# Respacing the state-space slots, a gelu on VectorE, and a new order at both ends of a one-core layer kernel

## The chip, the cores and the metric

The kernel runs on one core of a Trainium2 chip. The metric is the device time of one execution in microseconds (us). TensorE multiplies matrices, VectorE and ScalarE work elementwise, GpSimd is a slower elementwise engine, and SyncE (SP) issues nearly all DMA transfers from one queue. Each engine takes its instructions in a fixed order and waits on semaphores for the others.

## What is computed

One layer of a streaming encoder on 1024 prompt rows, 16 meta rows and 32 sample rows, all of width 1024, in fp32. The parts that matter here, cut from the reference:

```
xn = rmsnorm(h, norm_mix);  z = xn @ w_in            # q, kv, rope key | u | gate a | gate b
y_ssm, hr, hi = s5_scan(u, h0_re, h0_im)             # 64 groups, complex diagonal state, y = Re(C h) + D u
s = gelu(y_ssm)
o_b = (s @ w_glu_v) * sigmoid(s @ w_glu_g)
merged = sigmoid(g_a) * o_a + sigmoid(g_b) * o_b     # o_a: latent attention
h = h + merged @ w_out
h = h + relu(rmsnorm(h) @ w_mlp_up)**2 @ w_mlp_down
```

## The kernel before

Activations lie as columns: a tile has 128 features on the partitions and 1056 or 1072 positions along the free axis. Every fp32 operand of a large product is split into a high and a low fp32r part (`split`, lines 183 and 186: ScalarE casts the high part, GpSimd or VectorE subtracts for the low part), and `lin_part` (L264) makes three products of each pair: high x high, high x low, low x high.

**Input stage.** The string `HEAD` writes the order of the first steps out by hand. `xN` loads row tile N, `lN` loads weight block N, `i` loads the identity, `g` spreads the norm's gain over the partitions, `n...` makes the norms of the tiles named, `mN` scales tile N, `tNq` transposes half q of tile N and splits it, `w` splits the next weight block, and `pCM` makes the products of column chunk C with weight block M.

**State-space stage.** The remaining weight blocks of `w_in` are units (`run_unit`); a unit has eight k steps of nine products. Eight blocks j of four group pairs pass through the steps `st0` to `st5` in slots, one unit to a slot:

- `st0`: loads of U, a table tb on GpSimd, and tables clm (`cl`) and wxt (`wx`) on VectorE (48 instructions)
- `st1`: eight transposes of wxt (L581), copies to W, sixteen small products (L592), a store of ext and eight loads of M
- `st2`: products of U and W (L617), then VectorE's scan, from A (L638) to hb (L650, L651)
- `st3`: products of M and U (L668) and of hb and clm (L673) into Y, stores, and a load back as yt
- `st4`, `st5`: gelu of yt, and its store

`START[j]` is the slot of `st0` of block j; the others follow 1, 2, 4, 5 and 6 slots later. Steps written as generators give way after every few instructions, and `lin_part` takes one piece of each before every k step of the unit. Tiles with few buffers tie the blocks together: two of clm, one each of wxt, W, tb and hb.

The text's order is not the order that runs. The tile framework orders each engine's instructions by a timeline of its own, with the text's order as priority, so an instruction that it takes for ready can move ahead of its slot.

**Last stage.** The down projection works on pairs n of 256 output columns (`pairs`). For each, seven products `prod(n, p)` go into the PSUM banks X (two buffers), Z and Y (one each), and `gather` adds a bank to `yacc` on VectorE (L1635). The last four pairs (28 to 31) are written out one pair later: `out_rows` transposes eight blocks into the bank Y (L1646), ScalarE copies them to `yo` (L1649), and SP stores them (L1650); `out_sample` does the same for the sample rows (L1661, L1663).

Of the kernel before, what the change touches and what calls it, by code (L numbers as in the profile page):

```python
# [10 lines left out]
F32 = mybir.dt.float32  # L11
# [3 lines left out]
AF = mybir.ActivationFunctionType  # L15
ALU = mybir.AluOpType
# [98 lines left out]
KENG = ['vpvpvpp', 'vvpppvv', 'vpvvvvv', 'vpppvpp']  # L115


HEAD = "g x0 x8 x1 i l0 x2 x3 l1 x4 x5 x6 x7 n081 m0 t00 m8 t01 t80 m1 t10 w t11 w p00 p01 n23 m2 t20 t21 m3 t30 t31 p10 p11 n4567 m4 t40 t41 m5 t50 t51 p20 p21 m6 t60 t61 m7 t70 t71 p30 p31"
CH0 = [(0, 268), (268, 268), (536, 268), (804, 268)]
START = [2 + int(2.6 * j) for j in range(8)]  # L120
G3 = [(0, 3), (3, 3), (6, 2)]
GQ = [(t0 * KQ, nt * KQ) for t0, nt in G3]
EPS = 1e-6
# [2 lines left out]
GELU_C = math.sqrt(2.0 / math.pi)  # L126
# [30 lines left out]
def tile_layer(ctx: ExitStack, tc: tile.TileContext, a: dict, o: list, dbg=None):  # L157
    nc = tc.nc
# [140 lines left out]
    with tc.tile_pool(reuse_waits="tile", name="s5", bufs=1) as sp, tc.tile_pool(reuse_waits="tile", name="sps", bufs=3, space=PSUM) as sps:  # L299
# [32 lines left out]
        X = {}  # L332
        spare = iter([("M", 2)] * 2 + [("U", 2)] * 2 + [("Y", 3)] * 3 + [("A", 1), ("Bt", 1)])

# [45 lines left out]

        for w in HEAD.split():
            op, i = w[0], [int(c) for c in w[1:]]
# [28 lines left out]
        with ExitStack() as _:  # L411
# [14 lines left out]
            V = nc.vector  # L426
# [262 lines left out]
            def st4(j):  # L689
                yt = hold[j]["yt"]  # L690
                w = sp.tile([128, NQT], F32, tag="Y", name="gw", bufs=3)
                nc.scalar.activation(w, yt, AF.Square)
                V.tensor_scalar(w, w, GELU_C * 0.044715, GELU_C, op0=ALU.mult, op1=ALU.add)
                nc.gpsimd.tensor_tensor(w, w, yt, ALU.mult)
                hold[j]["w"] = w

            def st5(j):
# [4 lines left out]
                put("y", j, yt)  # L702
                put("s", j, w)

            slot = 2
            while slot <= START[7] + 6:
                steps = []
                for j in range(8):
                    for f, d in ((st5, 6), (st4, 5), (st3, 4), (st2, 2), (st1, 1), (st0, 0)):
                        if slot == START[j] + d:  # L710
                            steps.append(f(j))

                steps = [s for s in steps if s is not None]
                if w_units:
                    run_unit(*w_units.pop(0), steps)
                for s in steps:
                    for _ in s:
                        pass
                slot += 1
# [675 lines left out]
    with tc.tile_pool(reuse_waits="tile", name="mg", bufs=1) as mg:  # L1395
# [23 lines left out]
        for m in range(8):  # L1419
# [19 lines left out]
            for c0, n, ps in lin2(wh, wl, lambda k, c0, n: mh_[:, k, c0:c0 + n], lambda k, c0, n: ml_[:, k, c0:c0 + n], 8):  # L1439
# [4 lines left out]
                                               op0=ALU.mult, op1=ALU.subtract)  # L1444
# [19 lines left out]
    for g in range(3):  # L1464
        pt = tpp.tile([128, 512], F32, tag="tp", name="tp")
        b = blk[4 * g:4 * g + 4]
        for c0, n in b:
            i = c0 // 128
            nc.tensor.matmul(pt[:, c0 - 512 * g:c0 - 512 * g + n], lhsT=y[:n, i:i + 1].to_broadcast([n, 128]),
                             rhs=ident[:n, :n], start=True, stop=True)  # L1470
        w = sum(n for _, n in b)
# [20 lines left out]
    mu = ctx.enter_context(tc.tile_pool(reuse_waits="tile", name="mu", bufs=1))  # L1492
    hid = {}
# [58 lines left out]
    def w_load(n):  # L1552
        if n < len(pairs):
            g, j = pairs[n]
            for e in range(2):
                c0 = 256 * j + 128 * e
                nc.sync.dma_start(raws[2 * (n % 2) + e][:, :512].rearrange("p (k m) -> p k m", k=4),
                                  wd[512 * order[g]:512 * order[g] + 512, c0:c0 + 128].rearrange("(k p) m -> p k m", p=128))
# [36 lines left out]
    yps = ctx.enter_context(tc.tile_pool(reuse_waits="tile", name="yps", bufs=1, space=PSUM))  # L1595
# [17 lines left out]
    def bank2(pool, tag):  # L1613
        return pool.tile([128, 2, 512], F32, tag=tag, name=tag)

    def prod(n, p, ps, first, halves=((0, 1),)):
        g, j = pairs[n]
        e, wb, i = OPS[p]
        (h_, l_), x = whl[2 * (n % 2) + e], place[(7 * g + i) % 12]
        for hs in halves:  # L1620
            for k in range(2):
                for q, (w, u) in enumerate(((h_, 0), (h_, 1), (l_, 0))):
                    for s in hs:
                        nc.tensor.matmul(ps[:, s, :HS], lhsT=w[:, 256 * wb + 128 * k:256 * wb + 128 * k + 128],  # L1624
                                         rhs=x[:, u, k, HS * s:HS * s + HS],
                                         start=(first and k == 0 and q == 0), stop=(k == 1 and q == 2), skip_group_check=True)
        if j == 3:
            blk_load(7 * g + i + 12)

    def gather(n, r, c, ps, hs=None):  # L1630
        y_ = yacc[2 * pairs[n][1] + r][:, HN * c:HN * c + HN].rearrange("p (s n) -> p s n", s=2)
        v = ps[:, :, :HS]
        if hs is not None:
            y_, v = y_[:, hs:hs + 1], v[:, hs:hs + 1]
        nc.vector.tensor_tensor(y_, v, y_, ALU.add)  # L1635
# [4 lines left out]
    spot = [0]  # L1640

    def out_rows(m, t0, nt, pool=yps, tag="Y"):
        pt = bank2(pool, tag).rearrange("p a (b c) -> p (a b) c", c=128)[:, :nt]
        yv = yacc[m].rearrange("p (t c) -> p t c", t=T)
        for t in range(nt):
            nc.tensor.transpose(pt[:, t], yv[:, t0 + t, 0:128], ident)  # L1646
        spot[0] ^= 1
        yo = mu.tile([128, 8, 128], F32, tag=f"hid{spot[0]}", name="yo")[:, :nt]
        nc.scalar.activation(yo, pt, AF.Copy)  # L1649
        nc.sync.dma_start(y_o[:, t0:t0 + nt, m * 128:(m + 1) * 128], yo)  # L1650

# [24 lines left out]
    for n in range(N):  # L1676
        last = n == N - 1
        later = w_sums(n + 1) if not last else None
        X = bank2(xps, "X")
        prod(n, 1, X, True)  # L1680
        gather(n, 0, 0, X)
        if not last:
            w_split(n + 1, 0)
            later()
        if is_out(n - 1):
            out_rows(2 * pairs[n - 1][1], 0, 8)
        Z = bank2(zps, "Z")
        prod(n, 5, Z, True)
        if n == 0:

            rest[0]()
            gather(n, 1, 1, Z)
            Y = bank2(yps, "Y")
            prod(n, 2, Y, True)
            rest[1]()
            gather(n, 0, 0, Y)
            w_split(n + 1, 1)
            w_load(n + 3)
            prod(n, 6, X, False)
            gather(n, 0, 1, X)  # L1700
            rest[2]()
            prod(n, 3, Z, False)
            gather(n, 0, 1, Z)
            rest[3]()
            prod(n, 7, X, False)
            gather(n, 1, 1, X)
            before = X
            fill(n)
            continue
        gather(n, 1, 1, Z)  # L1710
        prod(n - 1, 4, before, False)
        gather(n - 1, 1, 0, before)
        if not last:
            w_split(n + 1, 1)
            w_load(n + 3)
        prod(n, 6, X, False)
        gather(n, 0, 1, X)
        if is_out(n - 1):
            out_rows(2 * pairs[n - 1][1] + 1, 0, 8)
        prod(n, 3, Z, False)  # L1720
        gather(n, 0, 1, Z)
        if is_out(n - 1):
            out_sample(n - 1)
        Y = bank2(yps, "Y")
        prod(n, 2, Y, True)
        gather(n, 0, 0, Y)
        prod(n, 7, X, False)
        gather(n, 1, 1, X)
        before = X
        if n < 3:  # L1730
            fill(n)
# [38 lines left out]
```

## Time and profile before

| | |
|---|---|
| median of 3 runs | 2052.73 us (2048.5 to 2053.4) |
| profiled execution | 2051.96 us, its span 2050.1 us |
| TensorE busy | 1992.4 us |
| VectorE, ScalarE, GpSimd busy | 1219.2, 765.8, 744.8 us |
| mean granted TensorE clock | 0.990 of full speed |

The span runs from the first to the last instruction of the profiled execution; the rest of its time lies around it. Busy time counts overlapping instructions of an engine once. The granted clock is the share of TensorE's full speed that the chip allowed.

### The profile page before, as it was taken

What the parts mean: (1) busy time and instruction counts of PE and PEld (TensorE: products, weight loads), DVE (VectorE), ACT (ScalarE), POOL (GpSimd) and SP (SyncE); (2) the same over time, 40 slices, a digit from 0 to 9 for tenths busy, and PEclk for the clock granted to TensorE, in tenths of its full rate; (3) what the DMA queues carried; (4) which work ended last, traced back from release to release, by engine and by line L of the source; (5) the groups of instructions that cost most, each with busy time, mean ns of one, the idle gap of its engine ahead of it and who ended that gap; (6) DMA issues with size and microseconds to landing.
All of it is one profiled execution on the core that took longest, in us unless ns stands there. A gap on an engine that the chain in (4) does not pass through costs nothing.

```text
span 2050.1 us, 35159 instructions
## 1 busy us (share of the span) xinstructions
PE 1992.4 (97%) x13328; PEld 1884.0 (92%) x13328; DVE 1219.2 (59%) x3092; ACT 765.8 (37%) x1691; POOL 744.8 (36%) x922
## 2 busy tenths in 40 slices
PE   7999999999999999999998999999999998999998
PEld 6988898899999888888887999999999998999997
DVE  5969776533756588988887444443444336444443
ACT  4213222223333467676765223333333332211112
POOL 0577676721222122121222001121221227767662
PEclk9999999999999999999999999999999999999999
DMA  5334444445343101110112634446555536765652
GB/s 146 115 110 126 126 132 131 122 128 184 120 150 118 55 12 27 18 28 17 24 20 87 196 102 126 132 153 225 200 207 224 196 141 236 293 241 195 250 197 85
DMA packets 269706, 276.62 MB, mean 135 GB/s; under 512 B 64602, under 2 KB 240433, under 8 KB 256994
## 3 DMA queue, kind: packets, MB, share of 16 engines
q1 hardware_dynamic: 269536, 274.38, 41.2%
q8 instruction: 105, 1.72, 0.3%
q14 instruction: 63, 0.52, 0.1%
q10 hardware_dynamic: 2, 0.00, 0.0%
HBM read 176.94 MB, written 97.39 MB: 134 GB/s over the span
## 4 chain that ended last, share of the span: by engine, by line
PE 82%; DVE 11%; DMA 3%; ACT 1%; POOL 1%; issue 1%; SPq 0%; ACTq 0%; DVEq 0%; POOLq 0%
PE acc L264 31%; PE pj L264 14%; PE X L1624 9%; PE Z L1624 4%; PE po L1279 3%; PE pj L1046 3%; PE pj L1111 3%; PE Y L1624 2%; PE pt L1254 1%; PE sp L673 1%; PE Sp L1197 1%; PE Sp L1189 1%; PE Sp L1190 1%; PE Sp L1192 1%; PE Sp L1191 1%
## 5 line engine op out<-in xcount | busy, mean ns | idle before, releaser
L186 POOL TENSOR_TENSOR wl<-raw,wh 128x1024 fp32r<-128x1024 f32 (+2 forms) x148 | 344.8, 2331 | 729.3 <-ACT wh L183 631.1
L183 ACT ACTIVATE wh<-raw 128x1024 fp32r<-128x1024 f32 (+2 forms) x166 | 169.1, 1019 | 696.9 <-PE acc L264 242.6
L264 PE MATMUL acc<-xh,wh 128*128 128x264 f32 (+6 forms) x736 | 189.3, 338 | 1.8 <-ACT xh L183 1.8
L264 PE MATMUL acc<-xh,wl 128*128 128x264 f32 (+4 forms) x736 | 181.5, 328 | 0.0
L264 PE MATMUL acc<-xl,wh 128*128 128x264 f32 (+5 forms) x736 | 181.5, 328 | 0.0
L1624 PE MATMUL X<-place,wh 128*128 128x264 f32 x1024 | 168.3, 287 | 2.1 <-ACT place L183 1.3
L1635 DVE TENSOR_TENSOR yacc<-X,yacc 128x528 f32<-128x528 f32 x129 | 90.4, 703 | 113.2 <-PE X L1624 113.0
L1624 PEld LDWEIGHTS X<-place,wh 128*128 128x128 f32 x1024 | 143.7, 191 | 2.7 <-ACT place L183 1.5
L264 PEld LDWEIGHTS acc<-xh,wh 128*128 128x128 f32 (+1 forms) x736 | 127.6, 191 | 14.3 <-issue 7.4
L264 PEld LDWEIGHTS acc<-xl,wh 128*128 128x128 f32 (+1 forms) x736 | 130.0, 190 | 2.1 <-issue 0.7
L264 PEld LDWEIGHTS acc<-xh,wl 128*128 128x128 f32 (+1 forms) x736 | 130.2, 191 | 1.9 <-issue 0.7
L1504 DVE SCALAR_TENSOR_TENSOR t<-acc,rstd 128x352 f32<-128x352 f32 x48 | 23.7, 522 | 150.5 <-PE acc L264 145.3
L1624 PE MATMUL X<-place,wl 128*128 128x264 f32 x512 | 104.7, 286 | 1.8 <-POOL wl L186 1.8
L264 PE MATMUL acc<-sh,wh 128*128 128x352 f32 x384 | 93.1, 325 | 0.6 <-ACT sh L749 0.6
L264 PE MATMUL acc<-sl,wh 128*128 128x352 f32 x384 | 93.6, 324 | 0.0
L264 PE MATMUL acc<-sh,wl 128*128 128x352 f32 x384 | 93.0, 324 | 0.0
L1624 PE MATMUL Z<-place,wh 128*128 128x264 f32 x512 | 84.5, 287 | 1.3 <-DVE yacc L1635 0.7
L1624 PEld LDWEIGHTS X<-place,wl 128*128 128x128 f32 x512 | 79.9, 190 | 2.0 <-POOL wl L186 2.0
L264 PE MATMUL pj<-ha,wh 128*128 128x352 f32 x360 | 79.1, 324 | 0.0
L264 PE MATMUL pj<-la,wh 128*128 128x352 f32 x360 | 78.7, 323 | 0.0
L264 PE MATMUL pj<-ha,wl 128*128 128x352 f32 x360 | 78.3, 323 | 0.0
L1279 PE MATMUL po<-ph,vt 128*128 128x256 f32 x320 | 74.3, 291 | 3.4 <-ACT ph L183 2.2
(483 smaller groups left out, 5294.4 us busy)
## 6 DMA issues: line engine op xcount, KB each, us to landing
bd<-place SPq DMA_DIRECT2D x49, 1056.0 KB
place<-bd SPq DMA_DIRECT2D x49, 1056.0 KB
raw<-in_w_mlp_up_dram SPq DMA_DIRECT2D x32, 512.0 KB
raw<-in_w_mlp_down_dram SPq DMA_DIRECT2D x64, 256.0 KB
raw<-in_w_in_dram SPq DMA_DIRECT2D x29, 512.0 KB
ud<-gst SPq DMA_DIRECT2D x8, 536.0 KB
U<-ud SPq DMA_DIRECT2D x64, 67.0 KB
yd<-Y SPq DMA_DIRECT2D x64, 66.0 KB
```

The source lines that it names most:

```text
L183: nc.scalar.activation(hi, src, AF.Copy)
L186: lo_eng.tensor_tensor(lo, src, hi.bitcast(F32), ALU.subtract)
L264: nc.tensor.matmul(pt[:M, :n], lhsT=w[:, k, :], rhs=x(k, c0, n), start=(k == 0 and p == 0), stop=(k == kt - 1 and p == 2),)
L673: nc.tensor.matmul(py[b][:, c], lhsT=cl[hs, q, pr, 1:9].rearrange("p a b -> p (a b)"), rhs=hb[hs, q, pr], start=False, stop=(q == 1),)
L1046: nc.tensor.matmul(ps[:R], lhsT=x[:, c, k0:k0 + R], rhs=w[:, c, :], start=(c == 0 and q == 0), stop=(c == 1 and q == 2))
L1111: nc.tensor.matmul(ps[:R, :384], lhsT=x[:, c, 128 * i:128 * i + R], rhs=w[:, c, :], start=(c == 0 and q == 0), stop=(c == 2 and q == 2))
L1189: nc.tensor.matmul(o_, lhsT=qh[:, h, 0, :R], rhs=kth[:, h, ks], start=True, stop=False)
L1190: nc.tensor.matmul(o_, lhsT=qh[:, h, 0, :R], rhs=ktl[:, h, ks], start=False, stop=False)
L1279: nc.tensor.matmul(po[:, :256], lhsT=w, rhs=x, start=st["first"], stop=(last and q == len(grp) - 1))
L1504: nc.vector.scalar_tensor_tensor(t, ps, 0.0, rstd[:, c], op0=ALU.max, op1=ALU.mult)
L1624: nc.tensor.matmul(ps[:, s, :HS], lhsT=w[:, 256 * wb + 128 * k:256 * wb + 128 * k + 128], rhs=x[:, u, k, HS * s:HS * s + HS], start=(first ...
L1635: nc.vector.tensor_tensor(y_, v, y_, ALU.add)
```

## The change

It does five things. `START` becomes 2, 5, 8, 10, 13, 15, 18, 20 (before: 2, 4, 7, 9, 12, 15, 17, 20). `st1` begins three k steps later in its slot when a step of an older block is in the same slot; in block 0, `st3` begins four k steps later and `st4` three. The inner gelu term is made by ScalarE (a square with a scale) and one VectorE instruction of two tensors, where it was a square, a VectorE instruction with two constants, and a GpSimd product. `HEAD` loads x2 ahead of weight block 0 and x4 ahead of block 1, and takes the second weight split behind the first products. In the last pair, product 2 goes ahead of product 6, and the row outputs rotate over three buffers instead of two.

```
-HEAD = "g x0 x8 x1 i l0 x2 x3 l1 x4 x5 x6 x7 n081 m0 t00 m8 t01 t80 m1 t10 w t11 w p00 p01 n23 ...
+HEAD = "g x0 x8 x1 i x2 l0 x3 x4 l1 x5 x6 x7 n081 m0 t00 t01 m8 m1 t80 t10 w t11 p00 w p01 n23 ...
...
-START = [2 + int(2.6 * j) for j in range(8)]
+START = [2, 5, 8, 10, 13, 15, 18, 20]
...
             def st4(j):
                 yt = hold[j]["yt"]
                 w = sp.tile([128, NQT], F32, tag="Y", name="gw", bufs=3)
-                nc.scalar.activation(w, yt, AF.Square)
-                V.tensor_scalar(w, w, GELU_C * 0.044715, GELU_C, op0=ALU.mult, op1=ALU.add)
-                nc.gpsimd.tensor_tensor(w, w, yt, ALU.mult)
+                nc.scalar.activation(w, yt, AF.Square, scale=math.sqrt(GELU_C * 0.044715))
+                V.scalar_tensor_tensor(w, w, GELU_C, yt, op0=ALU.add, op1=ALU.mult)
                 hold[j]["w"] = w
...
+            def late(n, f, j):
+                for _ in range(n):
+                    yield
+                yield from f(j) or ()
+
             slot = 2
             while slot <= START[7] + 6:
                 steps = []
                 for j in range(8):
                     for f, d in ((st5, 6), (st4, 5), (st3, 4), (st2, 2), (st1, 1), (st0, 0)):
                         if slot == START[j] + d:
-                            steps.append(f(j))
+
+                            n = 3 if f is st1 and steps else {st3: 4, st4: 3}.get(f, 0) if j == 0 else 0
+                            steps.append(late(n, f, j) if n else f(j))
...
-        spot[0] ^= 1
-        yo = mu.tile([128, 8, 128], F32, tag=f"hid{spot[0]}", name="yo")[:, :nt]
+        spot[0] = (spot[0] + 1) % 3
+        yo = mu.tile([128, 8, 128], F32, tag=("hid0", "hid1", "tA")[spot[0]], name="yo")[:, :nt]
...
         if not last:
             w_split(n + 1, 1)
             w_load(n + 3)
+        else:
+            Y = bank2(yps, "Y")
+            prod(n, 2, Y, True)
+            gather(n, 0, 0, Y)
         prod(n, 6, X, False)
         gather(n, 0, 1, X)
...
-        Y = bank2(yps, "Y")
-        prod(n, 2, Y, True)
-        gather(n, 0, 0, Y)
+        if not last:
+            Y = bank2(yps, "Y")
+            prod(n, 2, Y, True)
+            gather(n, 0, 0, Y)
         prod(n, 7, X, False)
         gather(n, 1, 1, X)
```

## Rows read from the trace of the kernel before

**Rows 1.** The page, part 1: busy us (share of the span) x instructions.

```profile
PE 1992.4 (97%) x13328; PEld 1884.0 (92%) x13328; DVE 1219.2 (59%) x3092; ACT 765.8 (37%) x1691; POOL 744.8 (36%) x922
```

**Rows 2.** Windows: stretch, length, busy us (instructions) by engine, granted clock, DMA share, GB/s.

```profile
0.00:25.00 25.00, 13.04 (x49) 9.30 (x50) 15.35 (x47) 16.84 (x29) 0.34 (x6) 1.00 1.01 263
131.95:137.00 5.05, 5.05 (x27) 4.33 (x27) 0.34 (x4) 0.52 (x3) 4.11 (x21) 0.53 0.31 78
250.00:258.00 8.00, 6.09 (x31) 5.58 (x29) 7.96 (x25) 1.86 (x5) 5.74 (x9) 0.79 0.33 135
381.00:389.00 8.00, 5.72 (x26) 5.35 (x25) 8.00 (x23) 3.24 (x6) 4.67 (x8) 0.81 0.16 66
400.00:500.00 100.00, 100.00 (x635) 94.45 (x634) 26.81 (x31) 28.18 (x57) 28.58 (x27) 1.00 0.44 136
```

**Rows 3.** TensorE's waits, whole span, last row 0 to 100: us, times, longest.

```profile
PE sp L581 <- DVE wxt L418: 5.4, 4, 2.3
PE sp L673 <- DVE hb L650: 4.2, 2, 4.0
...
PE sp L581 <- DVE wxt L418: 0.2, 1, 0.2
```

**Rows 4.** Timeline, block 0's scan and its reader: start, us, instruction [idle before].

```profile
117.56 1.29 DVE L638 TENSOR_TENSOR A<-xs,tb 128x1088 f32<-128x1088 f32 x1 [3.63 <-POOL tb L418]
...
131.95 0.81 PE L673 MATMUL sp<-hb,clm 64*128 64x132 f32 x4 [4.00 <-DVE hb L650]
```

**Rows 5.** Timeline of TensorE, slot of block 4's `st1` and block 3's `st3`.

```profile
252.20 0.33 PE L581 MATMUL sp<-ident,wxt 128*128 128x128 f32 x1 [1.91 <-DVE wxt L418]
...
257.46 0.72 PE L673 MATMUL sp<-hb,clm 64*128 64x132 f32 x8
```

**Rows 6.** Timeline of VectorE and GpSimd ahead of that.

```profile
241.84 2.84 DVE L693 TENSOR_SCALAR gw<-gw 128x1056 f32<-128x1056 f32 x1
...
245.80 2.48 DVE L416 TENSOR_TENSOR clt<-pw,bbar 128x128 f32<-128x128 f32 x1
...
255.75 0.16 DVE L651 TENSOR_TENSOR hb<-A,Bt 128x16 f32<-128x16 f32 x1
...
244.76 3.38 POOL L694 TENSOR_TENSOR gw<-gw,yt 128x1056 f32<-128x1056 f32 x1 [0.65 <-DVE gw L693]
```

**Rows 7.** Groups by form, VectorE, 60 to 420: busy us, mean ns, idle before.

```profile
L416 DVE TENSOR_TENSOR clt<-pw,bbar 128x128 f32<-128x128 f32 x32 | 17.2, 537 | 0.0
...
L700 DVE SCALAR_TENSOR_TENSOR gw<-gw,yt 128x1056 f32<-128x1056 f32 x6 | 7.4, 1240 | 0.0
```

**Rows 8.** Timeline of VectorE: first of block 5's 48 table instructions, and their successor.

```profile
266.49 0.62 DVE L418 TENSOR_TENSOR clm<-clt 128x144 f32<-128x144 f32 x2 [0.87 <-PE sp L673]
...
283.43 0.71 DVE L693 TENSOR_SCALAR gw<-gw 128x1056 f32<-128x1056 f32 x1
```

**Rows 9.** Timeline of ScalarE and VectorE in the input stage.

```profile
9.71 1.06 ACT L183 ACTIVATE wh<-raw 128x1024 fp32r<-128x1024 f32 x1 [0.68 <-DMA raw<-in_w_in_dram]
...
10.79 1.23 DVE L186 TENSOR_TENSOR wl<-raw,wh 128x1024 fp32r<-128x1024 f32 x1 [0.86 <-ACT wh L183]
...
12.78 1.28 DVE L363 SCALAR_TENSOR_TENSOR X<-X,r1y,gbc 128x1024 f32<-128x1024 f32 x1
```

**Rows 10.** The end: two copies of ScalarE's timeline, then the chain that ended last.

```profile
2032.72 1.03 ACT L1649 ACTIVATE yo<-Y 128x1024 f32<-128x1024 f32 x1 [8.22 <-PE Y L1646]
...
2040.92 1.02 ACT L1649 ACTIVATE yo<-Z 128x1024 f32<-128x1024 f32 x1 [4.64 <-PE Z L1646]
...
2037.23 1.73 PE Y L1624 x12
...
2039.75 1.11 PE Z L1646 x8
...
2042.60 3.88 DMA out_dram<-yo
2046.59 0.38 ACT yo L1649
```

More of the change, by code (lines that the diff above doesn't have):

```diff
@@ L115 @@
 KENG = ['vpvpvpp', 'vvpppvv', 'vpvvvvv', 'vpppvpp']
-HEAD = "g x0 x8 x1 i l0 x2 x3 l1 x4 x5 x6 x7 n081 m0 t00 m8 t01 t80 m1 t10 w t11 w p00 p01 n23 m2 t20 t21 m3 t30 t31 p10 p11 n4567 m4 t40 t41 m5 t50 t51 p20 p21 m6 t60 t61 m7 t70 t71 p30 p31"
+HEAD = "g x0 x8 x1 i x2 l0 x3 x4 l1 x5 x6 x7 n081 m0 t00 t01 m8 m1 t80 t10 w t11 p00 w p01 n23 m2 t20 t21 m3 t30 t31 p10 p11 n4567 m4 t40 t41 m5 t50 t51 p20 p21 m6 t60 t61 m7 t70 t71 p30 p31"
 CH0 = [(0, 268), (268, 268), (536, 268), (804, 268)]
-START = [2 + int(2.6 * j) for j in range(8)]
+START = [2, 5, 8, 10, 13, 15, 18, 20]
 G3 = [(0, 3), (3, 3), (6, 2)]
```

## The prediction

> **What bounds the kernel now.** The page comes first: TensorE is busy 97% of the span [rows 1]. Nothing in the change takes a product away, so it can win only what TensorE does not use: about 58 us of idle time in all, and the stretches in which its granted clock is low. The second view is the windows of the span [rows 2]. In a full stretch, 400 to 500 us, a product passes every 100 / 635 = 0.157 us at a granted clock of 1.00. In three stretches of the state-space stage the granted clock is under 1: 0.53 over 5.05 us, 0.79 over 8 and 0.81 over 8. That is the lower of two levels, 1.2 instead of 2.4 GHz, for part of each, and each stretch follows a TensorE wait. The third view says what those waits are [rows 3]: 5.4 us on wxt, VectorE's tables for the next block, before the transposes of `st1` (L581), and 4.2 us on hb, VectorE's scan result, before the output products of `st3` (L673). The reader is to see that a wait costs twice: once itself, and once in the slow clock after it. The price after it is 5.05 x 0.47 = 2.4, 8 x 0.21 = 1.7 and 8 x 0.19 = 1.5 us, 5.6 in all [rows 2].
>
> **Where the waits come from.** With `START` as it is, blocks 2, 4 and 7 come three slots after their predecessor, which itself came two after its own. In those places VectorE gets the predecessor's `st2` and the block's own `st0` in one stretch, and `st1` stands at the very head of the next slot. These are the three long wxt waits; a fourth, 0.2 us, belongs to block 0 and stays [rows 3]. The hb wait is nearly all block 0: VectorE starts its scan only when GpSimd's table is there, at 117.56, and TensorE stands 4.00 us until 131.95 [rows 4].
>
> **The new slots.** Only blocks 4 and 6 still come three slots after a pair that was two apart. Wherever an older block has a step in the slot, `st1` is put behind three k steps: 3 x 9 x 0.157 = 4.2 us at least [rows 2], more than any wxt wait (2.3 at most [rows 3]). In block 0 `st3` is put behind four k steps, 36 x 0.157 = 5.7 us; `st1` of block 1 moves from the slot before it into the same slot, which brings the slot's head forward by its eight transposes and sixteen small products: 8 x 0.33 = 2.6 us for the transposes by the longest row [rows 5], which overlap, so 2 us is my estimate for all. So hb is asked for some 3.7 us later against a wait of 4.00: gone within half a us. Removed: 5.4 + 4.2 - 0.2 = 9.4 of waits and 5.6 of slow clock, 15.0 us.
>
> **What is late next.** hb itself. In block 4's place the transposes got their tables at 252.20 after 1.91 us, and the old block's hb products followed at 257.46 [rows 5]; VectorE had written hb at about 255.9 [rows 6]. Without the wait and its slow clock TensorE would have come there 1.9 + 1.7 = 3.6 us sooner, at 253.9, 2 us before hb. Delaying `st1` alone would only hand the wait on. What may pull hb forward is the gelu edit. Its GpSimd product takes 3.38 us, and the VectorE instruction that starts inside it takes 2.48 [rows 6] where its kind has a mean of 0.54 [rows 7]: 1.9 us given back. VectorE pays 1.24 for the two-tensor form where the one-tensor form takes 0.71 undisturbed [rows 7, 8], so 0.5 more; it comes out 1.4 us ahead, hb at 254.5 against 253.9. The remaining wait is then 0.6 us in each of two places (blocks 4 and 6; the third place is gone). But the new form can be held up by GpSimd's weight splits as the old one was (2.84 in [rows 6]), and then it is 2 us with a slow clock of 1.6 behind it. Between 0.6 and 3.6 I take 1.5 each, 3 in all. State-space stage: 15.0 - 3 = 12 us gained; bounds 15 and 15.0 - 7.2 = 7.8.
>
> The row shows the one-tensor form at 0.71 and the two-tensor form at 1.24 us [rows 7, 8]. The Trainium skill ("VectorE: DVE Perf Modes", the perf-mode tier table) says that fp32 tensor-scalar work runs at twice the rate of any two-tensor operation; the trace agrees, 1.24 to 0.71. By that rule alone the gelu edit costs VectorE 8 x 0.53 = 4.2 us and gives nothing back, and hb comes later, not sooner: rival 1 below. The same skill ("SBUF — State Buffer", two separate sides) says that GpSimd and VectorE take turns at a shared port pair, a whole instruction at a time, which is what 2.48 beside 3.38 looks like; by that rule the edit pays.
>
> **Other moved steps.** What moves with `st0` of blocks 1, 2, 4 and 6 (eight loads of U each on SP, the tables on GpSimd) moves one slot, and is read two slots later. A later `st1` issues its store of ext and eight loads of M on SP's queue 4 us later; M is read three slots on, and a slot's 72 products alone take 11.3 us, so this is hidden. Its copies of W on ScalarE end some three k steps before the next slot reads them. `st4` of block 0 goes behind three k steps because yt now comes a little later; were it not, the weight casts behind it on ScalarE would wait. GpSimd loses eight products of 3.4 us, and the weight splits behind them come sooner; no TensorE wait in this stage names them, so I count nothing. The cover is the weight split one unit ahead; without it each would be a wait of up to 3.4 us.
>
> **Input stage.** Now ScalarE stands until 9.71 for the first weight block, and VectorE stands 0.86 us behind it and then makes that block's low part (1.23) in the middle of the norm that the first scaled rows need; those begin at 12.78 [rows 9]. The new order loads x2 before that block and x4 before the second, and splits the second block only behind the first products. If the split falls behind the norm, the first products come up to 0.86 + 1.23 = 2.1 us sooner; if the engines keep their order, all wait for a block that lands one load later, 512 KB at 263 GB/s, 2.0 us [rows 2]. VectorE has work without a pause after 12.78, so that only its idle 0.86 is likely to be won: I take 0.7.
>
> **The end.** The single "Y" bank passes from the rows of pair 30, copied from 2032.72 on, through their second half and the sample rows to the last pair's product 2, which starts only at 2037.23 [rows 10]. Every other product is done by then. Placed before the other two, it can start when that first copy ends, 2033.75: 3.5 us sooner. The next row transposes still queue behind it, and behind ScalarE's copies, so the copy that began at 2040.92 begins at about 2038.4: product and addition take 2039.75 - 2037.23 = 2.5 us and end at 2036.3, then come the other rows' transposes and copy, 1.0 each. Its store needs about 3.9 us [rows 10]; in the new rotation of three buffers the last copy waits for that store, the one before it for an older one. The copy that was at 2046.59 then starts at 2038.4 + 1.0 + 3.9 = 2043.3, 3.3 us sooner, and the last store goes with it. Bounds: 1 (the third buffer alone helps one copy) and 4.7 (the last copy too is free of its wait).
>
> **Sum.** 12 + 0.7 + 3.3 = 16.0 us. The profiled execution took 2051.96 (its span is 2050.1, 1.86 lie around it); the median of the runs shown is 2052.73, 0.8 above. 2051.96 - 16.0 = 2036.0. About 0.3%, 6.2 us, is what a measurement of this kernel can tell from no change.
>
> **Rivals.** (1) The waits only move: VectorE pays 0.5 us a block for the two-tensor form and gets nothing back, hb is late in the two places, something else in the third, each with its slow clock. Then block 0's 4.0 + 2.4 and the end's 3.3 remain: 2051.96 - 9.7 = 2042.3. For it speaks that hb stood 2 us behind wxt; against it the third pattern, which is gone. (2) The edits change little: the order in the trace is not that of the text alone (block 5's `st0` begins at 266.49 [rows 8], a slot and more ahead of its place), so new slots could give the old order. Then the end's 3.3 and small change remain: about 2048.5, within 0.3%. Against it: `st1` and `st3` stood exactly at their slots' heads. (3) Slower: block 1's tables. `st0` of block 1 now stands a slot behind `st2` of block 0. If VectorE takes them in that order it waits for GpSimd until 117.56, ends the scan at 131.95 [rows 4] and needs 17.0 us for the tables [rows 8], until 149; TensorE asks for them at about 129.5. A wait of 19.5 and 2 of slow clock make 2036 + 21.5 = 2057.5. It decides from a start of the tables later than 112.5, and makes the kernel slower once that start is some 14 us later still. Against it: VectorE has nothing else to do before 117.56, and wrote these tables ahead of their slot before.
>
> **How the numbers follow.** The forecast 0.64 (2030 to 2041), rival 1 0.15 (2040 to 2046), rival 2 0.12 (2046 to 2054), rival 3 0.09 (2054 to 2060). Faster 0.79, same 0.12, slower 0.09. The low end: 15 + 2.1 + 4.7 = 21.8 gained, 2030. The high end, 2047, takes in rival 1 and the top of the next and leaves out no more than 2 in 10.
>
> **What would show it.** Right: no wxt wait over 0.5 us behind block 0; no hb wait at block 0; a granted clock of 1.00 from 100 to 400 us; hb waits of 1 to 2 us at blocks 4 and 6 at most; product 2 of the last pair before the second row transposes; at most one long wait of ScalarE on a store at the end. Wrong: a new TensorE wait over 5 us at block 1 or 2, or the wxt waits at their old size.

## The result, and the profile after

The changed kernel takes 2036.78 us (median of 4 runs, 2033.65 to 2036.92) against 2053.05 for the kernel before on the same chip (4 runs, 2048.5 to 2053.4). The ratio is 0.9922 with a 95% interval of 0.9905 to 0.9939: faster, by 16.3 us or 0.8%. The forecast was 2036.0, with 2030 to 2047 as its range.

The page of the profiled execution (2036.92 us, span 2035.1, mean granted clock 0.996), its busy row, which answers to [rows 1]:

```profile
PE 1983.2 (97%) x13328; PEld 1878.1 (92%) x13328; DVE 1211.5 (60%) x3092; ACT 766.2 (38%) x1691; POOL 718.1 (35%) x914
```

TensorE makes as many products in 9.2 us less busy time: that is slow clock that is gone. GpSimd has eight instructions and 26.7 us less.

Three marks divide the span into parts that can be compared: the first transpose of ld (the end of the input stage), the first transpose of fin (the end of the state-space stage), and ScalarE's first copy of pair 30's rows. Before they stand at 52.10, 473.13 and 2032.72 us, after at 50.92, 458.81 and 2020.26. The parts, in us:

| | input stage | state-space stage | between | end |
|---|---|---|---|---|
| before | 52.10 | 421.03 | 1559.59 | 17.38 |
| after | 50.92 | 407.89 | 1561.45 | 14.84 |
| gained | 1.2 | 13.1 | -1.9 | 2.5 |

The windows view over the state-space stage of each kernel, before first (columns as in [rows 2]):

```profile
52.10:473.13 421.03, 411.30 (x2766) 379.42 (x2766) 283.05 (x699) 111.12 (x271) 264.92 (x465) 0.98 0.42 123
```

```profile
50.92:458.81 407.89, 404.85 (x2765) 376.37 (x2765) 276.40 (x699) 111.91 (x271) 238.19 (x457) 1.00 0.43 127
```

The length less TensorE's busy time is its idle time: 9.7 us before and 3.0 after. So the stage won 6.7 us of waits and 6.4 us of product time. The waits of TensorE after, from 50 to 475 us, against [rows 3]:

```profile
PE sp L673 <- DVE hb L650: 2.5, 1, 2.5
PE sp L581 <- DVE wxt L418: 0.5, 1, 0.5
```

One wait on hb is left, and it is not where the forecast put it. TensorE's timeline shows it at block 1, and the windows behind it show what it costs in clock:

```profile
173.28 0.72 PE L673 MATMUL sp<-hb,clm 64*128 64x132 f32 x8 [2.50 <-DVE hb L650]
```

```profile
173.28:179.00 5.72, 5.71 (x33) 5.12 (x34) 0.23 (x3) 0.00 (x0) 4.85 (x21) 0.70 0.15 64
179.00:184.00 5.00, 5.00 (x35) 4.50 (x35) 0.00 (x0) 1.17 (x3) 4.53 (x12) 1.00 0.43 116
```

5.72 x 0.30 = 1.7 us: part of that stretch went at 1.2 instead of 2.4 GHz. Everywhere else from 100 to 460 us the granted clock is 1.00, and at the places of blocks 4 and 6 TensorE waits for nothing.

### The profile page after: what moved, and what is told of

Read it like the earlier page. It is cut to its first block, busy times and chain, and to the rows that moved or that the text cites. A ratio compares the mean times of both kernels' runs of the same rounds, so it can differ in the third digit from the quotient of the medians.

```text
span 2035.1 us, 35117 instructions
## 1 busy us (share of the span) xinstructions
PE 1983.2 (97%) x13328; PEld 1878.1 (92%) x13328; DVE 1211.5 (60%) x3092; ACT 766.2 (38%) x1691; POOL 718.1 (35%) x914
## 4 chain that ended last, share of the span: by engine, by line
PE 88%; DVE 5%; DMA 3%; ACT 2%; POOL 1%; issue 1%; SPq 0%; ACTq 0%; DVEq 0%; POOLq 0%
PE acc L264 37%; PE pj L264 14%; PE X L1630 9%; PE Z L1630 4%; PE po L1285 3%; PE pj L1052 3%; PE pj L1117 3%; PE Y L1630 2%; PE pt L1260 1%; PE sp L673 1%; PE Sp L1203 1%; PE sp L617 1%; PE Sp L1195 1%; PE Sp L1196 1%; PE Sp L1198 1%; PE Sp L1197 1%
## 5 line engine op out<-in xcount | busy, mean ns | idle before, releaser
L1641 DVE TENSOR_TENSOR yacc<-X,yacc 128x528 f32<-128x528 f32 x129 | 90.4, 702 | 112.7 <-PE X L1630 112.5
```

## The experiments

The dispute is over which edit made the stage faster: the new slots with their delays, or the gelu edit, which the prediction used only to bring hb forward by 1.4 us. And for the gelu edit: is it the form of VectorE's instruction, or the GpSimd product that is gone? All runs are compared with the kernel before on the same chip. "Stage" is the state-space stage between the two marks; idle is its length less TensorE's busy time.

| kernel | time, us (runs) | stage | busy | idle | waits on wxt; hb |
|---|---|---|---|---|---|
| before | see above | 421.03 | 411.30 | 9.73 | 5.4; 4.2 |
| delays alone | 2049.07 (1) | 420.35 | 408.18 | 12.17 | 0.5; 5.0 |
| new slots and delays, old gelu | 2051.67 (10) | 416.65 | 407.44 | 9.21 | 0.5; 8.7 |
| gelu alone | 2042.06 (1) | 410.58 | 406.02 | 4.56 | 0.5; 4.0 |
| slots, delays and gelu | 2037.70 (4) | 407.80 | 404.73 | 3.07 | 0.5; 2.5 |
| new gelu and an idle GpSimd product | 2053.35 (10) | 417.21 | 407.02 | 10.19 | 6.0; 4.2 |
| old form, product on VectorE | 2044.92 (1) | 411.32 | 405.81 | 5.51 | 1.1; 4.4 |
| changed kernel | 2036.78 (4) | 407.89 | 404.85 | 3.04 | 0.5; 2.5 |
| changed kernel without delays | 2041.49 (1) | 411.61 | 405.33 | 6.28 | 0.5; 5.8 |
| changed kernel, `st3` of block 1 later | 2032.49 (5) | 403.36 | 402.83 | 0.53 | 0.5; 0 |

The times come from more than one chip, so that kernels are compared by their ratios to the kernel before and by the stage. A single time says little: in thirteen of the fourteen profiles (the last experiment says what is wrong with the other) the stretch "between", which no edit touches, takes from 1558.7 to 1564.3 us. The stage's length is steadier: the two kernels below that change only the last pair show 422.57 and 421.41 against 421.03.

**New slots and delays with the old gelu.** The new `START` and the delayed steps are in; gelu, load order and end are as before.

```
-START = [2 + int(2.6 * j) for j in range(8)]
+START = [2, 5, 8, 10, 13, 15, 18, 20]
...
+                            n = 3 if f is st1 and steps else {st3: 4, st4: 3}.get(f, 0) if j == 0 else 0
+                            steps.append(late(n, f, j) if n else f(j))
```

> The kernel before with the new slots and the delayed steps alone; the gelu keeps its GpSimd product, both ends stay old. If the gelu edit is what pulls hb forward (the prediction), hb is late without it: TensorE waits of 2 us or more on hb, each with its slow clock, at blocks 3 and 5 (read in the slots of blocks 4 and 6) and a longer one than 2.5 at block 1, so 2053 - 13 + 3 x 3 = about 2049. If the new slots alone do the work, the waits are those of the changed kernel, one of 2.5 us, and the time is 2053 - 13 = 2040.

2051.67 us, ratio 1.0001 (0.9989 to 1.0014): no change. TensorE's waits:

```profile
PE sp L673 <- DVE hb L650: 8.7, 3, 4.1
PE sp L581 <- DVE wxt L418: 0.5, 1, 0.5
```

The wxt waits are gone, and nearly the same time is now waited for hb, in three places: 4.12 us (block 1), 3.38 us (at 346.56) and 1.18 us (at 262.01), the last of them shorter than the 2 us that was expected. Without the gelu edit the slots only exchange one wait for the other. The profile's stage is 4.4 us shorter; the median of ten runs does not show it, and its interval of about 2.7 us either way has no room for it.

**The same with the new gelu.** Slots, delays and gelu; the ends are as before.

> The kernel before with the slots, the delayed steps and the gelu on VectorE; both ends stay old. By the changed kernel's trace the state-space stage gives 13 us: 2053 - 13 = 2040. If the input stage and the end carry more of the 16 us than the trace says (1.2 and 2.5), this stays above 2042.

2037.70 us, ratio 0.9937 (0.9922 to 0.9952). The stage, 407.80, and the waits, 2.5 on hb and 0.5 on wxt, are those of the changed kernel. So the stage's part of the change is these three edits, and the gelu edit decides what the other two are worth.

**The delays alone.** The old `START`, with the later `st1`, `st3` and `st4`.

> The kernel before with the delayed steps alone: old slots, old gelu. The prediction says that a later st1 only hands the wait on: no wxt wait over 0.5 us, block 0's hb wait gone, but hb waits of 1 to 2 us where wxt was late (blocks 1, 3 and 6), each with a slow clock; block 0's 6.4 us and little else are gained, about 2045. If the place of st1 was all, nothing takes the wxt waits' place: 2053 - 15 = 2038.

```profile
PE sp L673 <- DVE hb L650: 5.0, 4, 2.3
PE acc L264 <- ACT gst L309: 4.8, 1, 4.8
PE sp L617 <- DVE ext L599: 1.8, 1, 1.8
PE sp L581 <- DVE wxt L418: 0.5, 1, 0.5
```

The step "delaying `st1` alone would only hand the wait on" stands: wxt falls to 0.5, and hb in four places, ext and a bank that ScalarE had to empty take its place; 12.1 us in all, more than before. The stage is 0.7 us shorter. The wait of 4.8 us on that bank was in no expectation, and the one time is 4 us above the 2045 that was expected.

**Gelu alone.** Only the three lines of `st4`.

> The kernel before with the gelu on VectorE alone. If VectorE gets back more from GpSimd's missing product than the two-tensor form costs (1.9 against 0.5), the wxt waits of 1.0, 1.9 and 2.3 shrink by about 1.4 each and lose their slow clock, block 0's 4.0 stays: about 2053 - 4 - 3 = 2046. If VectorE only pays, the wxt waits grow by 0.5 each: 2054.

2042.06 us in one run, with 2050.24 for the kernel before (13 runs); the stage takes 410.58, 10.4 less than before. That is a larger gain than the 2046 that was expected. The waits:

```profile
PE sp L673 <- DVE hb L650: 4.0, 1, 4.0
PE sp L581 <- DVE wxt L418: 0.5, 1, 0.5
```

All three long wxt waits are gone, with the slots as they were; only block 0's wait on hb is left. This is the finding of the study: the edit that the forecast used as a helper does most of the work. VectorE's and GpSimd's timelines at block 4's place, the stretch of [rows 6], show how:

```profile
228.39 1.01 DVE L418 TENSOR_TENSOR clm<-clt 128x144 f32<-128x144 f32 x4 [15.76 <-PE sp L673]
...
238.22 1.23 DVE L693 SCALAR_TENSOR_TENSOR gw<-gw,yt 128x1056 f32<-128x1056 f32 x1
239.37 1.28 DVE L644 TENSOR_TENSOR_SCAN Gs<-L,A 128x544 f32<-128x544 f32 x1
240.57 2.42 DVE L416 TENSOR_TENSOR clt<-pw,bbar 128x128 f32<-128x128 f32 x1
...
246.56 0.28 DVE L418 TENSOR_TENSOR wxt<-clt 128x128 f32<-128x128 f32 x1
```

```profile
238.70 4.13 POOL L186 TENSOR_TENSOR wl<-raw,wh 128x1024 fp32r<-128x1024 f32 x1 [8.33 <-ACT wh L183]
```

From the first table instruction to the last of wxt VectorE needs 246.84 - 228.39 = 18.5 us. In the kernel before the same stretch runs from 230.78 to 252.14, 21.4. Of the 2.9 us, 1.6 are the gelu instruction itself (1.23 against 2.84 in [rows 6]) and 1.0 the first four table instructions (1.01 against 2.02 before). The instruction that the prediction counted on, the one of 2.48 us beside GpSimd's product [rows 6], is still held here, for 2.42: now by the weight split. At block 7's place it is not. VectorE's and GpSimd's rows there, the kernel before first, then gelu alone:

```profile
374.20 2.85 DVE L693 TENSOR_SCALAR gw<-gw 128x1056 f32<-128x1056 f32 x1
...
378.17 2.50 DVE L416 TENSOR_TENSOR clt<-pw,bbar 128x128 f32<-128x128 f32 x1
...
373.21 3.27 POOL L186 TENSOR_TENSOR wl<-raw,wh 128x1024 fp32r<-128x1024 f32 x1 [5.18 <-ACT wh L183]
...
377.12 3.39 POOL L694 TENSOR_TENSOR gw<-gw,yt 128x1056 f32<-128x1056 f32 x1 [0.65 <-DVE gw L693]
```

```profile
366.16 3.39 DVE L693 SCALAR_TENSOR_TENSOR gw<-gw,yt 128x1056 f32<-128x1056 f32 x1
...
370.67 0.26 DVE L416 TENSOR_TENSOR clt<-pw,bbar 128x128 f32<-128x128 f32 x1
...
365.11 3.32 POOL L186 TENSOR_TENSOR wl<-raw,wh 128x1024 fp32r<-128x1024 f32 x1 [5.11 <-ACT wh L183]
```

With gelu alone the gelu instruction stands beside the split, and the table instruction passes in 0.26 us. Block 2's place is like it (2.83 and 2.50 before, 3.39 and 0.26 with gelu alone). So in each of the three places two VectorE instructions were held before, one beside the weight split and one beside the product; without the product one is held, whichever the split meets. The two take 5.3 us together before and 3.65 after, at all three places: 1.7 us less, with the longer two-tensor form already paid. The whole stretches are 2.0, 2.9 and 2.8 us shorter at blocks 2, 4 and 7, where the wxt waits were 1.0, 1.9 and 2.3.

**The new gelu with an idle product.** GpSimd gets its work back, as two products of 480 columns each that nobody reads.

```
+                scr = sp.tile([128, 480], F32, name="scr", tag="scr")
+                for c in (0, 480):
+                    nc.gpsimd.tensor_tensor(scr, w[:, c:c + 480], yt[:, c:c + 480], ALU.mult)
```

> The kernel before with the gelu on VectorE, and GpSimd made to form two products of 480 columns (960 of the old 1056) from the same two tiles at the same place, into a tile that nobody reads. If GpSimd's product held VectorE up, VectorE gets its 2.2 us a block back no more, wxt comes late again (1 to 2 us in three places, each with a slow clock), and the time is 2042 + 8 = about 2050. If only the new form of VectorE's instruction counts, which is not held up behind a weight split (1.24 against 2.84), the wxt waits stay under 0.6 us and the time at 2042.

2053.35 us, ratio 1.0005 (0.9992 to 1.0018): by the time the whole gain is undone. The stage of the one profile, 417.21, is longer than with gelu alone by 6.6 us of the 10.4. TensorE's waits are those of before again:

```profile
PE sp L581 <- DVE wxt L418: 6.0, 4, 2.0
PE sp L673 <- DVE hb L650: 4.2, 2, 4.0
```

The same place in VectorE's and GpSimd's timelines:

```profile
241.13 3.39 DVE L693 SCALAR_TENSOR_TENSOR gw<-gw,yt 128x1056 f32<-128x1056 f32 x1
...
245.65 1.25 DVE L416 TENSOR_TENSOR clt<-pw,bbar 128x128 f32<-128x128 f32 x1
...
247.46 1.71 DVE L418 TENSOR_TENSOR wxt<-clt 128x128 f32<-128x128 f32 x3
```

```profile
240.42 2.99 POOL L186 TENSOR_TENSOR wl<-raw,wh 128x1024 fp32r<-128x1024 f32 x1 [5.46 <-ACT wh L183]
...
244.60 2.15 POOL L696 TENSOR_TENSOR scr<-gw,yt 128x480 f32<-128x480 f32 x1 [1.20 <-DVE gw L693]
```

Beside the two halves of the product, of 2.15 and 1.26 us, VectorE's table instructions stand again: 1.25 us where the same one passed in 0.26 at block 7 above, and 1.71 for the three that take 0.68 there.

The waits do not bring all of the slow clock back: over some 5 us behind the wxt waits at blocks 2, 4 and 7 (1.91, 1.84 and 2.04 us) the granted clock is 1.00, 0.67 and 1.00, where the kernel before has 1.00, 0.64 and 0.65. The windows behind block 7's wait, before first, then here:

```profile
384.58:389.00 4.42, 4.42 (x17) 4.42 (x18) 4.42 (x16) 0.60 (x1) 4.36 (x6) 0.65 0.29 119
```

```profile
383.04:388.00 4.96, 4.96 (x36) 4.44 (x38) 4.96 (x19) 0.60 (x1) 4.88 (x3) 1.00 0.27 109
```

So a wait does not always cost twice, and that is part of what this profile's stage keeps.

At block 4's place, in the rows above, the weight split began 0.71 us ahead of VectorE's gelu instruction, which then took 3.39 us; with gelu alone it began 0.48 us behind it, and it was the split that took longer, 4.13. The mean of the gelu instruction over its seven places is 2.17 us here, 1.86 with gelu alone and 1.55 in the changed kernel. The Trainium skill ("SBUF — State Buffer", two separate sides) says that of a VectorE instruction with two inputs in SBUF and a GpSimd one, the one that starts first has the shared port pair for its whole length and the other stands still; these two pairs of rows agree.

**The old form with the product on VectorE.** The one-tensor instruction stays, and VectorE makes the product that GpSimd made, so it bears one instruction more than before.

```
-                nc.gpsimd.tensor_tensor(w, w, yt, ALU.mult)
+                V.tensor_tensor(w, w, yt, ALU.mult)
```

> The kernel before with the old gelu's last product moved from GpSimd to VectorE: VectorE keeps the one-tensor instruction and gets a two-tensor one more, 1.24 us. If GpSimd's product was what held VectorE up (2.2 us), VectorE gains 1 us a block: wxt waits shrink to 0 to 1.3, about 2046. If the one-tensor form's collision with the weight split was, VectorE only pays: wxt waits of 2.2 to 3.5, about 2055.

2044.92 us in one run; the stage takes 411.32, 0.7 more than with gelu alone. At the same place the one-tensor instruction still takes 2.84 us behind a split, and the product adds 1.25, but the table instruction of 2.48 us passes in 0.26, the stretch takes 20.2 us, 1.2 less than before, and the wxt waits shrink to 1.1. With the run above it answers the question: it is GpSimd's product that had to go, whatever form VectorE's part has.

**The changed kernel without its delays.** All steps stand at the heads of their slots.

```
-                            n = 3 if f is st1 and steps else {st3: 4, st4: 3}.get(f, 0) if j == 0 else 0
+                            n = 0
```

> The changed kernel with all its steps at the heads of their slots: new slots, new gelu, new ends, but no k steps of delay anywhere. It tells what the delays are worth once the gelu edit is in. My theory: the gelu edit has removed the three long wxt waits, so what the delays still cover is small: block 0's wait on hb of 4.0 comes back with its slow clock of 2.4, and one of the wxt waits by up to 1 us; the stage then takes 411 to 415 us against 407.9, and the kernel about 2042. Rival, that the delays alone do the work at the new slots: the three wxt waits come back at 1.5 to 2 us each with their slow clock, 418 us or more. A third case, that the delays do nothing at the new slots: 408, and 2037.

2041.49 us in one run; the stage takes 411.61, at the low edge of what was expected. No wxt wait returns; one wait on hb does:

```profile
130.56 1.25 PE L673 MATMUL sp<-hb,clm 64*128 64x132 f32 x8 [5.76 <-DVE hb L650]
```

So behind the gelu edit the delays of `st1` cover nothing that is still there: the one wait that returns is block 0's, and with it the stage is 3.7 us longer. It is longer than before (5.76 against 4.00), as hb is asked for sooner at the new slots: at 130.56 - 5.76 = 124.80 us, against 131.95 - 4.00 = 127.95 [rows 4]. Of these 3.2 us, 0.9 are the earlier end of the input stage (51.16 against 52.10); 2.2 are left, where the prediction had put 2 for the moved `st1` of block 1. Against gelu alone (410.58, with the old slots) this kernel's stage is 1.0 us longer: behind the gelu edit the new `START` by itself gains nothing. Whether block 0's delays would do their part at the old slots was not tried.

**Block 1's `st3` later.** If the one wait that is left has the cause of block 0's, the same cure must work. The changed kernel, with `st3` of block 1 behind three k steps and its `st4` behind three:

```
-                            n = 3 if f is st1 and steps else {st3: 4, st4: 3}.get(f, 0) if j == 0 else 0
+                            n = 3 if f is st1 and steps else {st3: 4 - j, st4: 3}.get(f, 0) if j < 2 else 0
```

> The changed kernel with st3 of block 1 three k steps and its st4 three k steps later in their slots, as in block 0 (four and three). If block 1's hb wait is of itself, 2.5 us and 1.75 of slow clock go and nothing takes their place: 2036.8 - 4.2 = 2032.6. If hb is late for the sake of what follows it, the later clm release delays block 3's tables and a wxt wait of 1 to 4 us appears there: no gain.

2032.49 us (5 runs, 2029.56 to 2034.97), ratio to the kernel before 0.9908 (0.9892 to 0.9924). The stage loses 4.5 us more, and nearly all of its idle time:

```profile
51.43:454.79 403.36, 402.83 (x2766) 374.60 (x2765) 276.67 (x699) 112.13 (x271) 239.48 (x457) 1.00 0.43 129
```

This version beats the kernel before. That it also beats the changed kernel rests on the stage of its profile: the intervals of the two ratios (0.9908 and 0.9922) overlap. It gives the stage a floor: 402.8 us of products when nothing waits.

**The old load order.** The changed kernel with the old `HEAD`.

> The changed kernel with the old order of the input stage. The changed kernel's first products began no sooner and stayed at the lower clock 3.6 us longer, but its later wait and its dip of the clock are gone, 1.2 us in all: 2036.8 + 1.2 = 2038 with the dip back at 30 to 40 us. If the input order is worth the 2.1 us that its parts promised, 2039; if chance sets the dip, 2037.

2039.49 us in one run. The first transposes of ld stand at 50.55 us, sooner than in the changed kernel (50.92); the 2.7 us by which the whole is longer lie in the stretch "between" (1564.3). Over the thirteen profiles the ten kernels with the old order show 50.26 to 52.52, mean 51.35; the three with the new one 50.92, 51.16 and 51.43, mean 51.17. By these means the new load order gains 0.2 us, and of the 1.2 in the table above most is scatter. The windows view says where the scatter is from, before first, then the old order in the changed kernel:

```profile
25.00:50.00 25.00, 22.13 (x163) 20.95 (x162) 12.62 (x24) 6.92 (x14) 0.00 (x0) 0.93 0.17 36
```

```profile
25.00:50.00 25.00, 23.07 (x175) 21.66 (x174) 12.96 (x25) 8.37 (x18) 0.00 (x0) 1.00 0.17 36
```

With the old order five of ten profiles have the dip to 0.93 here, and they are the five late ones (51.70 to 52.52); the five without it end at 50.26 to 50.73. None of the three with the new order has it. If the new order does keep the dip away, it also costs half a us where there is none; three profiles don't settle that.

**The last pair's order alone, and the third buffer alone.** Each is put into the kernel before by itself.

> The kernel before with only the last pair's product 2 ahead of product 6; the row outputs still rotate over two buffers. It tells whether the end's gain of 2.5 us comes from the order or from the third buffer. My theory: the order. Product 2 starts about 3.5 us sooner than before, right behind the first copy of pair 30's rows, and the next row transposes no longer stand behind it; but with two buffers the copies meet their stores sooner, and ScalarE's waits on stores grow. From the first row transposes of pair 30 to the end of the span 16.5 to 17.5 us, against 18.5 before and 15.97 in the changed kernel. Rival, that the order gains nothing without the third buffer: 18 or more. The input stage has the old load order: first transposes of ld at 50.3 to 52.5 us, as in the eight runs with that order.

> The kernel before with only the third buffer for the row outputs; the products keep their order. From the first row transposes of pair 30 to the end of the span: if the third buffer by itself frees only one copy, 17.5 us or so, 1 less than before (18.5); if the chain through product 2 alone sets the end, no change, 18.5. Product 2 stays where it was, some 4.5 us behind the first copy's start. First transposes of ld at 50.3 to 52.5 us.

Both are single runs (2052.01 and 2055.41 us), so only the end is read: from ScalarE's first copy of pair 30's rows to the end of the span. Seven kernels with the old end show 17.04 to 17.49 us, mean 17.22. The order alone shows 16.45, the buffer alone 16.33, both together 14.84 to 14.89 in the four kernels that have them. So the order brings 0.8, the buffer 0.9, and both 2.4, more than their sum; of the order alone I had expected more than of the buffer. The chain that ended last with the order alone, in its last pieces:

```profile
2038.76 1.03 ACT yo L1649
...
2039.81 3.66 DMA out_dram<-yo
...
2043.58 0.61 ACT yo L1649
...
2044.20 2.35 DMA out_dram<-yo
...
2046.66 0.38 ACT yo L1649
```

Product 2 is early, but two of the last copies stand behind stores that must free their buffer. With the buffer alone the end of the chain begins with the late product 2 and still has one such store:

```profile
2041.68 1.75 PE Y L1624 x12
...
2046.39 3.55 DMA out_dram<-yo
...
2050.05 0.38 ACT yo L1649
```

Each edit alone runs into the wait that the other one shortens.

**Five buffers.** The version with block 1's later `st3`, whose three short row outputs take two further buffers.

```
+        if nt < 8:
+            yo = wp.tile([128, 1152], F32, tag="raw", name="yo", bufs=2)[:, :128 * nt].rearrange("p (t c) -> p t c", c=128)
+        else:
+            yo = mu.tile([128, 8, 128], F32, tag=("hid0", "hid1", "tA")[spot[0]], name="yo")[:, :nt]
```

> The changed kernel with st3 of block 1 three k steps later, and with two more buffers for the short row outputs, so that no copy of ScalarE at the end waits for a store. If the two waits left at the end (1.46 and 1.48 us) are what sets it, the span ends about 2 us sooner: from the first row transposes of pair 30 to the end 14 us against 15.97, and a median some 2 us below that of the kernel with the late step alone. Rival: the stores' own bandwidth sets the end (the stores queue behind each other whoever frees the buffer), and the gain is under 0.5 us; then the chain ends in stores, not in a copy. The state-space stage takes 403 to 404 us from the transposes of ld to those of fin, as in the kernel with the late step alone (403.4), against 407.9 in the changed kernel.

Ratio 0.99 (0.9883 to 0.9916), against 0.9908 with three buffers: the intervals cover each other, so a gain of 2 us is neither shown nor excluded. One of the five executions took 6679.81 us, with 40.64 us for 72 products on TensorE where the changed kernel takes 11.54, and it is the one that was profiled; so no view of it is compared, and whether the last copies still wait stays open. The other four took 2029.82 to 2035.73 us.

## Why the prediction was right, and where it was not

**The total** came out: 16.0 us forecast, 16.3 measured. **The state-space stage** was forecast at 12 and is 13.1. That these are so near is in part luck. Against the version without waits (403.36) the stage before has 17.7 us to lose, where the prediction counted 15.0; the changed kernel still has 4.5 of them, where it left 3. And the gain has another cause than the one that the sum was made from.

**The step that failed is the use of the gelu edit.** The prediction let the slots and delays remove the 15.0 us and gave the gelu edit only the 1.4 us a place by which hb, next in line, comes sooner. That a later `st1` alone would hand the wait on it said itself, and the runs agree: slots and delays without the gelu edit move the waits from wxt to hb, and the median stays at 2051.67. What it did not ask is what the gelu edit does to the wxt waits themselves, with the old slots. Alone it takes 10.4 us out of the stage, all three long wxt waits among them. The mechanism, that GpSimd's product holds VectorE up, was right, and its net price nearly so: 1.4 us a place forecast, 1.7 measured on the two instructions that were held. The rest of the 2.0 to 2.9 us a place lies mostly in the first table instructions (the first four take 1.00, 1.01 and 1.55 us at blocks 2, 4 and 7 against 1.33, 2.02 and 1.80; the fifth at block 7 0.31 against 0.85). At block 4 GpSimd's own table pieces end 4.9 us behind the start of these instructions in the kernel before and 2.0 behind it with gelu alone. That this is what slows them is my reading; the runs show the shift, not its cause. Each of the three stretches became shorter by more than its wxt wait, and so the waits went without any new slot.

**The remaining waits** were forecast as 3 us at blocks 4 and 6. There are none there; there is one at block 1, 2.5 us and 1.7 of slow clock, 4.2 together. The prediction gave block 0's `st3` a delay of 36 products against its wait and did not ask the same of block 1, whose hb comes from the next scan behind it. The experiment that delays it gains 4.5 in the stage.

**The price of the slow clock** was 5.6 us from three stretches [rows 2]. Against the floor of 402.8 the stage before has 8.5 us too much product time. The three stretches were read rightly; the other 2.9 us lie in no row that I found, and stay open.

**Rival 1** (2042.3) fell with the price that it rests on. The two-tensor form does take 1.23 us where nothing holds it, against 0.71 for the one-tensor form. The Trainium skill ("VectorE: DVE Perf Modes", the perf-mode tier table) gives fp32 work with one tensor twice the rate of work with two; the rows show 1.7 times. But the form is not what is paid for: the old form with the product on VectorE, which gives VectorE an instruction more than any other version, keeps 9.7 of the 10.4 us. **Rival 2**, that the new slots give the old order, is answered by the first experiment: the slots do move the waits, from wxt to hb.

**Rival 3** is excluded: no wait in the changed kernel is over 2.5 us in the stage, and wxt waits only once, 0.5. VectorE writes block 1's wxt at 99.57 to 100.76, before the 112.5 at which that rival begins.

**The input stage** was put at 0.7 and is 0.2 at most. ScalarE makes the weight cast later, as thought, and the scaling starts at 11.21 instead of 12.78 [rows 9]. VectorE's and TensorE's rows:

```profile
11.21 3.67 DVE L363 SCALAR_TENSOR_TENSOR X<-X,r1y,gbc 128x1024 f32<-128x1024 f32 x3 [0.23 <-ACT gbc L391]
```

```profile
20.40 0.82 PE L264 MATMUL acc<-xh,wh 128*128 128x268 f32 x2 [1.69 <-ACT xh L183]
```

But the first products begin at 20.40, only 0.3 us sooner than before (20.66): they now wait 1.69 us for a high part that ScalarE makes behind the squares of two other row tiles, at 17.65 and 18.71. The step followed VectorE and forgot who else must come first on ScalarE. From there the products also pass slowly for longer, one in 0.22 us until 27.6 us and one in 0.12 after that, where before the pace rose at 24.0. The expectation above called this the lower clock; the granted clock reads 1.00 in both stretches, so the cause of the pace is not shown.

**The end** was put at 3.3, with bounds of 1 and 4.7, and is 2.5, or 2.4 by the mean of the seven old ends. The order is as forecast: product 2 starts 1.4 us behind that first copy (2021.67), where it was 4.5 behind before. What was too small is the time from the copy of bank Z to the last copy, which waits for that copy's store: 3.9 us in the prediction. ScalarE's timeline, and a piece of the chain that ended last:

```profile
2030.06 0.38 ACT L1655 ACTIVATE yo<-X 128x256 f32<-128x256 f32 x1 [1.46 <-DMA out_dram<-yo]
2031.92 0.38 ACT L1655 ACTIVATE yo<-Z 128x256 f32<-128x256 f32 x1 [1.48 <-DMA out_dram<-yo]
```

```profile
2027.67 4.15 DMA out_dram<-yo
```

The copy of bank Z ended at 2026.20 + 1.02 = 2027.22. Its store was issued 0.45 us later, behind a store of sample rows in SP's queue, and took 4.15, so that the last copy began 4.7 us behind it: 0.8 more than forecast, which is what is missing from the 3.3. The copy ahead of it waits too, as the prediction had it, for 1.46 us; the sign "at most one long wait" was therefore not met.

## What to carry to other kernels

Where a slow engine holds up a faster one, count all the instructions that stand in the stretch in which both work, not the one that is looked at: in the three places here each of GpSimd's two long instructions held one of VectorE's, and taking one away freed one, whichever it was. Before respacing a schedule to hide a wait, ask the same question of the next operand in the chain; a delay only helps when the thing waited for does not itself come later, and a cure that fits one block should be tried on its neighbour. Read the gain of a stage between two marks in its own profile, and collect the same marks from several runs before giving a us to an edit.

## What was not expected

- After a wait of some 2 us the granted clock fell in some places and not in others: 1.00 behind the 2.04 us at block 7 with the idle product, 0.65 behind the 2.28 us there in the kernel before. What decides is not shown.
- Two edits of the end gain 0.8 and 0.9 us alone and 2.4 together.
- GpSimd's weight split, beside which two VectorE instructions passed one behind the other (1.23 and 1.28 us), took 4.13 us where the median of 23 such splits from 60 to 420 us is 2.40 in the same run. By these numbers it stood still for 1.7 us, about as long as both took from its start (238.70 to 240.57), and got on only when the second one was done; the third instruction then stood behind it and took 2.42.
- The stretch of 1,560 us in which no edit does anything varies by 5.6 us from profile to profile, a third of what the change gains.
